# Five small edits to the order of work in a two-layer encoder kernel: pooling products issued later, one split issued a step later, weight splits on two engines, a second PSUM bank for spread scales, and the last two tiles finished in halves

## The chip, the cores and the metric

The kernel runs on one core of one Trainium2 chip. The metric is device time in microseconds of one execution of the whole program, given as the median of three timed runs. The engines carry the names of the profile: PE is TensorE's matmul pipe and PEld its weight load, DVE is VectorE, ACT is ScalarE, POOL is GpSimd, and SP is the queue that issues most transfers.

## The reference, cut to what matters

Two request groups, a prompt of 2048 rows and a sample of 512, pass through the same two layers of width 1024:

```python
h = rms_norm(x, pre_g)
u, zp, q, k, v, za = jnp.split(h @ w_in, SPLIT_POINTS, axis=-1)
pool_out = multiscale_pool(u, pool_w, pool_scale) * silu(zp)   # 4 groups: (window mean - u) @ pool_w[g]
q, k = rope(q), rope(k)
# per head two softmax maps: a = softmax(q0 k0) - lam * softmax(q1 k1); o = a @ v, RMSNorm per head
attn_out = diff_attention(q, k, v, lam, subln_g, lambda_init) * silu(za)
y = jnp.concatenate([pool_out, attn_out], axis=-1) @ w_out
x = x + rms_norm(y, post_g)
```

## The kernel before

Every float32 operand of a product is split into a high part (a copy rounded to the matmul's format, mostly on ACT) and a low part (source minus high part, on DVE or POOL), and products are made of two or three matmuls of parts. The function `split` (L111 the high part, L116 the low part) does both. Each layer has three stages.

**Projection.** `stream` (L279, L251) multiplies 512-row blocks (`hth`, `htl`) by 256-column slices of the weight (`wh`, `wl`), kind by kind in the order u, zp, k, v, q, za, each first for the prompt's blocks 0 and 1, then for 2 and 3. `evacuate` takes results out of PSUM. Every matmul yields to a scheduler, `advance`, which in one of three turns takes a single step of a generator `pool_block`. There are 20 pooling groups in a layer (five blocks, four window sizes), one after the other. A group loads `u` from device memory, adds windows on POOL (tiles `sum`, L367, up to four passes, then edge fixes at L372 and L375), subtracts on DVE (`df`, L379), splits `df` into `dhl` (ACT, then DVE), lets nine steps pass, does three matmuls into PSUM bank `mm` (L387), scales (L390), splits into `hl` and stores. The tiles `u`, `z`, `df` and `dhl` have one buffer each, so the `u` of one group is loaded after the `df` of the group ahead of it is done. When the projection's last matmul for the prompt has been issued, a loop `while q: drop(q)` issues whatever of the pooling generators is left.

**Attention.** Steps of four score products (L442, L443, tiles `sc`), maxima on DVE (L453), exponentials on ACT (L469), combination of the two maps on POOL (L484, L485), transposes on PE with splits (`tr`, `ath`, `atl`, L494), products with v (`ot`, L511). `fill` puts other matmuls in between: the sample's last projections into bank `mm`, then the pooled half of the output projection (L702), whose weights `load_wout` splits when they arrive: rows of 1024 columns, high parts `woh` on ACT, low parts `wol` on DVE for the first four, POOL in halves for the last four. Near the end `fill.first` advances `first_outputs`, which spreads the per-row scales of the first tiles over 128 columns (`spread`, L747), rescales (`rescale`, L751), splits, and starts the attention half of the output projection.

**Output.** `phase3` goes over 20 tiles of 128 rows. For each it spreads scales into bank `mm`, rescales into `mixs`, splits into `hl` (ACT and POOL), multiplies by the output weights (L757), adds to the pooled half (`y`, L803), and `post` normalizes: square sum on ACT (L842), power on POOL (L846), scaling on DVE (L848), residual add on POOL (L850), store. In the last layer the last tile goes through `post_half` in two halves (L819 to L830); the tile ahead of it uses the short pauses `QUICK`.

PE, ACT, DVE and POOL execute in the order in which this code issues (`manual_schedule`); SP's order is chosen by the framework. The eight PSUM banks are four `sc`, two `tr`, one `ot`, one `mm`.

Of the kernel before, what the change touches and what calls it, by code (L numbers as in the profile page):

```python
# [11 lines left out]
F32 = mybir.dt.float32  # L12
# [8 lines left out]
P = 128  # L21
# [3 lines left out]
H = 4  # L25
# [8 lines left out]
FILL = 6  # L34
AGAIN = 2
RAW = 6
FAST = 1
SLOW = 3
LATER = 8
ONE = 2  # L40
# [12 lines left out]
def f32(ap):  # L53
    return ap.bitcast(F32)
# [3 lines left out]
def trunk_kernel(ctx: ExitStack, tc: tile.TileContext, a, outs):  # L58
# [14 lines left out]
    def bank(tag):  # L73

        taken[tag] += 1
        return psum.tile([P, TB], F32, name=f"{tag}{taken[tag] % BANKS[tag]}")
# [272 lines left out]
    def pool_block(c, st, tb, u_p, t_p, tag):  # L349

        S = st["S"]
        for g, w in enumerate(WINDOWS):
            u = u_p.tile([P, TB + 2 * HALO], F32, name="u", bufs=1)
            lo_t, hi_t = tb * TB - HALO, (tb + 1) * TB + HALO
            a0, a1 = max(lo_t, 0), min(hi_t, S)
            if a0 > lo_t:
                nc.gpsimd.memset(u[:, :HALO], 0.0)
            if a1 < hi_t:
                nc.gpsimd.memset(u[:, TB + HALO :], 0.0)
            nc.sync.dma_start(u[:, a0 - lo_t : a1 - lo_t], st["us"][g][:, a0:a1])  # L360
            z = u_p.tile([P, TB], F32, name="z", bufs=1)
            nc.sync.dma_start(z, st["zs"][g][:, tb * TB : (tb + 1) * TB])
            j0, cur, step = HALO - w // 2, u, 1
            while step < w:
                n = TB + w - 2 * step
                nx = u_p.tile([P, TB + 2 * HALO], F32, name="sum")
                nc.gpsimd.tensor_tensor(nx[:, j0 : j0 + n], cur[:, j0 : j0 + n], cur[:, j0 + step : j0 + step + n], op=ALU.add)  # L367
                cur, step = nx, 2 * step
                yield
                yield  # L370
            if a0 > lo_t:
                nc.gpsimd.tensor_tensor(cur[:, j0 : j0 + HALO], cur[:, j0 : j0 + HALO], efix[:, g, :HALO], op=ALU.mult)  # L372
            if a1 < hi_t:
                e0 = j0 + TB - HALO
                nc.gpsimd.tensor_tensor(cur[:, e0 : e0 + HALO], cur[:, e0 : e0 + HALO], efix[:, g, HALO:], op=ALU.mult)  # L375
            yield
            yield
            df = u_p.tile([P, TB], F32, name="df", bufs=1)
            nc.vector.scalar_tensor_tensor(df, cur[:, j0 : j0 + TB], 1.0 / w, u[:, HALO : HALO + TB], op0=ALU.mult, op1=ALU.subtract)  # L379
            yield  # L380
            d = u_p.tile([P, 2, TB], F32R, name="dhl", bufs=1)
            split(d[:, 0], d[:, 1], df, nc.scalar, nc.vector)
            for _ in range(9):
                yield
            ps = bank(tag)
            for i, (pw, m) in enumerate((("pwh", 0), ("pwl", 0), ("pwh", 1))):
                nc.tensor.matmul(ps, lhsT=c[pw][:, g, :], rhs=d[:, m], start=i == 0, stop=i == 2)  # L387
            yield
            mx = u_p.tile([P, TB], F32, name="df", bufs=1)
            nc.vector.scalar_tensor_tensor(mx, ps, c["psc"][:, g : g + 1], z, op0=ALU.mult, op1=ALU.mult)  # L390
            yield
            hl = t_p.tile([P, 2, TB], F32R, name="hl")
            split(hl[:, 0], hl[:, 1], mx, nc.scalar, nc.vector)
            nc.sync.dma_start(st["mp"][:, g, :, tb * TB : (tb + 1) * TB], f32(hl))

    def attention(c, p, po, fill):
# [156 lines left out]
        def block(st, h, qb, ks, vs, q=None):  # L553
            nch = st["S"] // TB
            b = dict(st=st, h=h, qb=qb, ks=ks, vs=vs, q=q or load_q(st, h, qb), sets=[])
            b["z"] = [None, None]
            b["g"] = p["o"].tile([P, QB], F32, name="g", bufs=2)
            nc.sync.dma_start(b["g"], st["gs"][h][:, qb * QB : (qb + 1) * QB])
            for qt in range(2):
                for m in range(2):  # L560
                    b["sets"].append(dict(b=b, qt=qt, m=m, nch=nch, ps=[], e=[]))
            jobs = [(s, ch) for s in b["sets"] for ch in range(nch)]
            for i in range(0, len(jobs), 4):
                yield jobs[i : i + 4]

        def blocks():

            nq, ns = pr["S"] // QB, sa["S"] // QB
            ahead = None
            for h in range(H):  # L570
                kv = load_head(pr, h)
                for qb in range(nq):
                    yield from block(pr, h, qb, *kv[:2], kv[2] if qb == 0 else None)
                    if h == H - 1:
                        n = qb
                        if qb == nq - 1:
                            fill.last()
                        if qb == 0:
                            fill.all()
                            ahead = load_head(sa, 0)  # L580
                        if n % ns == 0:
                            skv = ahead
                        if qb == nq - 1:
                            fill.first(1)
                        yield from block(sa, n // ns, n % ns, *skv)
                        if n % ns == 0 and n // ns + 1 < H:
                            ahead = load_head(sa, n // ns + 1)

# [91 lines left out]
    def load_wout(l, p, wo, ks, raws, pools):  # L680

        for k in ks:
            raw = raws.pop(0)
            wp = p["wop" if k < GROUPS else "woa"]
            wo["h", k] = wp.tile([P, D], F32R, name=f"woh{k}")
            wo["l", k] = wp.tile([P, D], F32R, name=f"wol{k}")
            if k < GROUPS:
                split(wo["h", k], wo["l", k], raw, nc.scalar, nc.vector)
            else:
                for ns in halves:  # L690
                    for _ in range(WGAP):
                        yield
                    split(wo["h", k][:, ns], wo["l", k][:, ns], raw[:, ns], nc.scalar, nc.gpsimd)
            if k + 2 < KT:
                raws.append(load_rows(l, k + 2, pools[k % 2]))
            if k < GROUPS:
                yield
# [48 lines left out]
            wide = st["rstat"][:, t, h : h + 1].to_broadcast([P, P])  # L746
            nc.tensor.transpose(ps[:, h * P : (h + 1) * P], wide, ident)  # L747

    def rescale(ps, src, m, hl, lo_eng):

        nc.vector.tensor_tensor(m, ps.rearrange("p (h n) -> p h n", h=H), src, op=ALU.mult)  # L751
        split(hl[:, 0], hl[:, 1], m, nc.scalar, lo_eng)

    def head_products(ps, hl, wo, ns):
        todo = [(hl[:, m, h, :], wo[w, GROUPS + h]) for h in range(H) for m, w in terms]
# [4 lines left out]
    def phase3(l, wo, scaling, pairs, early, ready, ph, mixed, kept, es, nxt):  # L760
# [22 lines left out]
        def scale(s):  # L783
            if s["hl"] is not None:
                return
            ps = bank("mm")
            spread(ps, s["st"], s["t"])
            yield
            s["hl"] = m_p.tile([P, 2, H, P], F32R, name="hl")
            rescale(ps, s["h"], m_p.tile([P, H, P], F32, name="mixs"), s["hl"], nc.gpsimd)  # L790
            yield

        def products(s):
# [19 lines left out]
        def post_half(s, ns):  # L813

            st, t, y = s["st"], s["t"], s["y"]
            if ns.start == 0:
                s["sy"] = small.tile([P, 2], F32, name="sy2")
            junk = y_p.tile([P, D], BF16, name="junk", bufs=1)
            nc.scalar.activation(junk[:, ns], y[:, ns], AF.Square, accum_out=s["sy"][:, ns.start // TB : ns.start // TB + 1])  # L819
            nc.vector.tensor_tensor(y[:, ns], y[:, ns], gpost[:, ns], op=ALU.mult)  # L820
            yield
            if ns.start:
                ss = small.tile([P, 1], F32, name="sy")
                nc.gpsimd.tensor_tensor(ss, s["sy"][:, 0:1], s["sy"][:, 1:2], op=ALU.add)
                nc.gpsimd.tensor_scalar(ss, ss, 1.0 / D, NORM_EPS, op0=ALU.mult, op1=ALU.add)
                rs = small.tile([P, 1], F32, name="ry")
                nc.gpsimd.tensor_tensor(rs, ss, mhalf[:, :1], op=ALU.pow)
                for ns in halves:
                    nc.vector.scalar_tensor_tensor(y[:, ns], y[:, ns], rs, s["x"][:, ns], op0=ALU.mult, op1=ALU.add)
                    nc.sync.dma_start(st["y"][t * P : (t + 1) * P, ns], y[:, ns])  # L830

        def post(st, t, s):
# [2 lines left out]
                    yield  # L835

            y = s["y"]
            lags = LAGS if nxt or len(tiles) < len(order) or s is not tiles[-2] else QUICK
            yield from pause(lags[0])
            junk = y_p.tile([P, D], BF16, name="junk", bufs=1)  # L840
            ss = small.tile([P, 1], F32, name="sy")
# [44 lines left out]
    class Layer:  # L886
# [60 lines left out]
        def run(self, posts, before):  # L947
# [145 lines left out]
            def first_outputs():  # L1093
# [3 lines left out]
                def prepare(t, m, hl):  # L1097
                    ps = bank("tr")
                    spread(ps, pr, t)
                    rescale(ps, pairs["p", t // 2 * 2 * P][:, :, t % 2 * P : (t % 2 + 1) * P], m, hl, nc.vector)  # L1100
                    ready["p", t] = hl
                    yield

# [123 lines left out]
```

## Time and profile before

| | |
|---|---|
| timed runs | 3168.99, 3148.02, 3166.07 us |
| median | 3166.07 us |
| profiled execution, own time | 3150.91 us |
| its span, first to last instruction | 3149.1 us |
| PE busy in the span | 3065.4 us |
| mean granted TensorE clock | 0.994 |

The profile's span is 1.8 us shorter than the execution's own time. The profiled execution lies near the fastest of the timed runs, 15.2 us below their median. A matmul's row gives a modelled duration, longer than the distance to the next matmul's start when they follow without a wait, so PE's work is counted by starts.

### The profile page before, as it was taken

Reading aid. Unit: us, or ns where it says so; the run is one execution under the profiler, and the core shown is the slowest. Engines: PE = TensorE matmul, PEld = TensorE weight load, DVE = VectorE, ACT = ScalarE, POOL = GpSimd, SP = SyncE. Lnnn points to the kernel's source line nnn. Section 1 sums busy time; section 2 is a strip of 40 time slices with the busy share of each in tenths; the row PEclk is TensorE's granted clock in tenths of the full one; section 3 lists DMA queues with packets and bytes.
Section 4 is the critical chain, followed back from the end, with each engine's and each line's share of the span. In section 5 each row is a group of like instructions: output and inputs, shape, how many; then the busy total and the mean of one; then the engine's idle time right before and its main releaser. Section 6 shows DMA issues by size and latency. Waiting matters only on the chain. (4 is left out here: it accounts for less than half of the span.)

```text
span 3149.1 us, 48450 instructions
## 1 busy us (share of the span) xinstructions
PE 3065.4 (97%) x17016; PEld 2585.4 (82%) x17016; DVE 2069.5 (66%) x3255; ACT 1719.1 (55%) x3915; POOL 1768.4 (56%) x1972
## 2 busy tenths in 40 slices
PE   8999999999998999998999999999999989999998
PEld 6898888778887888887778888897788878888876
DVE  3354255688888887775634543556888888877754
ACT  3244233377777777763333442333777777777632
POOL 1000122289997888885710002222999978878766
PEclk9999999999999999999999999999999999999999
DMA  5354357653424434436854544577424243344367
GB/s 203 116 158 151 124 161 205 197 151 94 124 67 120 122 97 142 128 104 223 307 170 121 158 137 131 170 202 220 134 85 121 65 136 106 108 137 123 101 224 257
DMA packets 298899, 464.53 MB, mean 148 GB/s; under 512 B 26144, under 2 KB 180768, under 8 KB 298656
## 3 DMA queue, kind: packets, MB, share of 16 engines
q1 hardware_dynamic: 292032, 439.42, 46.8%
q10 hardware_dynamic: 6624, 22.02, 1.8%
q8 instruction: 134, 2.20, 0.3%
q14 instruction: 109, 0.89, 0.1%
HBM read 293.57 MB, written 167.77 MB: 146 GB/s over the span
## 5 line engine op out<-in xcount | busy, mean ns | idle before, releaser
L453 DVE TENSOR_REDUCE mx<-sc 128x1 f32<-128x512 f32 x1024 | 650.1, 684 | 185.4 <-PE sc L443 185.2
L469 ACT ACTIVATE e<-sc,nm 128x512 f32<-128x512 f32 x1088 | 732.4, 694 | 32.2 <-DVE nm L456 28.5
L485 POOL TENSOR_TENSOR e<-e,e 128x1024 f32<-128x1024 f32 (+1 forms) x288 | 664.5, 2307 | 24.0
L279 PE MATMUL sc<-hth,wh 128*128 128x512 f32 x1408 | 556.1, 395 | 1.1 <-ACT wh L111 1.0
L279 PE MATMUL sc<-htl,wh 128*128 128x512 f32 x1408 | 554.7, 394 | 0.2 <-DVE htl L116 0.2
L279 PE MATMUL sc<-hth,wl 128*128 128x512 f32 x1408 | 553.2, 393 | 0.5 <-DVE wl L116 0.5
L111 ACT ACTIVATE ath<-tr 128x512 fp32r<-128x512 f32 x544 | 329.3, 606 | 252.1 <-PE ot L511 190.7
L442 PE MATMUL sc<-ks,q 128*128 128x512 f32 x1024 | 433.9, 424 | 3.3 <-ACT e L469 3.1
L443 PE MATMUL sc<-ks,q 128*128 128x512 f32 x1024 | 406.0, 397 | 0.0
L116 DVE TENSOR_TENSOR atl<-tr,ath 128x512 fp32r<-128x512 f32 x544 | 364.9, 682 | 25.7 <-ACT ath L111 25.5
L511 PE MATMUL ot<-ath,v 128*128 128x256 f32 x2176 | 368.7, 291 | 6.7 <-DVE mt L521 6.7
L494 PEld LDWEIGHTS tr<-ident,e 128*128 128x128 f32 x2176 | 266.3, 141 | 98.1 <-DVE atl L116 27.4
L494 PE MATMUL tr<-ident,e 128*128 128x128 f32 x2176 | 328.7, 274 | 18.1 <-DVE atl L116 14.6
L484 POOL TENSOR_SCALAR e<-e,nco 128x1024 f32<-128x1024 f32 (+1 forms) x288 | 329.9, 1145 | 14.9
L169 POOL TENSOR_TENSOR rs<-ss,mhalf 128x1 f32<-128x1 f32 x40 | 25.6, 639 | 552.6 <-DVE ss L167 552.6
L511 PEld LDWEIGHTS ot<-ath,v 128*128 128x128 f32 x2176 | 310.5, 190 | 30.4 <-DVE mt L521 9.2
L279 PEld LDWEIGHTS sc<-hth,wl 128*128 128x128 f32 x1408 | 264.7, 188 | 60.3 <-DVE wl L116 1.1
L279 PEld LDWEIGHTS sc<-hth,wh 128*128 128x128 f32 x1408 | 264.9, 188 | 59.9 <-ACT wh L111 1.4
L279 PEld LDWEIGHTS sc<-htl,wh 128*128 128x128 f32 x1408 | 265.0, 188 | 57.7 <-DVE htl L116 0.5
L442 PEld LDWEIGHTS sc<-ks,q 128*128 128x128 f32 x1024 | 193.8, 189 | 64.7 <-ACT e L469 38.3
L116 DVE TENSOR_TENSOR wl<-wr,wh 128x1024 fp32r<-128x1024 f32 x94 | 121.0, 1289 | 183.0 <-ACT wh L111 183.0
L469 ACT ACTIVATION_READ_ACCUMULATOR e<-sc,nm 128x1 f32 x1088 | 231.5, 213 | 0.0
(156 smaller groups left out, 5725.2 us busy)
## 6 DMA issues: line engine op xcount, KB each, us to landing
wr<-in_w_in SPq DMA_DIRECT2D x128, 512.0 KB, 4.1
q<-qs_p SPq DMA_DIRECT2D x128, 256.0 KB, 4.1
ks_p<-hl SPq DMA_DIRECT2D x64, 256.0 KB, 3.4
vs_p<-hl SPq DMA_DIRECT2D x128, 128.0 KB, 2.5
qs_p<-hl SPq DMA_DIRECT2D x64, 256.0 KB, 3.5
mp_p<-hl SPq DMA_DIRECT2D x32, 512.0 KB, 3.8
ks<-ks_p SPq DMA_DIRECT2D x64, 256.0 KB, 6.0
v<-vs_p SPq DMA_DIRECT2D x32, 512.0 KB, 5.8
```

The costliest lines, as they stand in the source:

```text
L111: nc.scalar.activation(hi, src, AF.Copy)
L116: lo_eng.tensor_tensor(lo, src, f32(hi), op=ALU.subtract)
L169: nc.gpsimd.tensor_tensor(rs, ss, mhalf[:, :1], op=ALU.pow)
L279: nc.tensor.matmul(ps, lhsT=w[k // 4][m][:, k % 4, ns], rhs=h[:, k, :], start=k + i == 0, stop=k == KT - 1 and i == 2)
L442: nc.tensor.matmul(ps, lhsT=q[:, m, 0, ts], rhs=kk, start=True, stop=False)
L443: nc.tensor.matmul(ps, lhsT=q[:, m, 1, ts], rhs=kk, start=False, stop=True)
L453: nc.vector.reduce_max(s["mx"][:, ch : ch + 1], s["ps"][ch], axis=AX.X)
L469: nc.scalar.activation(dst, s["ps"][ch], AF.Exp, bias=s["nm"], accum_out=s["b"]["z"][s["qt"]][:, m, ch : ch + 1])
L484: nc.gpsimd.tensor_scalar(x1[:, :n], x1[:, :n], nco, 0.0, op0=ALU.mult, op1=ALU.add)
L485: nc.gpsimd.tensor_tensor(x0[:, :n], x0[:, :n], x1[:, :n], op=ALU.add)
L494: nc.tensor.transpose(ps[:, j, qt * P : (qt + 1) * P], e[kt // 8][:, kt % 8 * P : (kt % 8 + 1) * P], ident)
L511: nc.tensor.matmul(b["ot"][:, :QB], lhsT=b["vs"][v][kt // 8][:, kt % 8, :], rhs=at[:, j, :], start=unit + i == 0, stop=kt == nkt - 1 and i ...
```

## The change

1. A pooling group lets 13 steps pass between splitting `dhl` and its three matmuls, where it let nine.
2. In `first_outputs` the split after `rescale` is issued one step later (the split is taken out of `rescale`, and a `yield` stands ahead of it). After the sample's last attention block `fill.first(1)` is called once more.
3. The low parts of the first four output weights are made in halves, one on DVE and one on POOL.
4. In `phase3` the spread scales alternate between banks `mm` and `ot`.
5. The last two tiles go through `post_half` (`FAST = 2`), the third from the end takes `QUICK`, and the last but one waits six more steps (`BEFORE`) before its final scaling.

```diff
-FAST = 1
+FAST = 2
+BEFORE = 6
...
             split(d[:, 0], d[:, 1], df, nc.scalar, nc.vector)
-            for _ in range(9):
+            for _ in range(13):
                 yield
...
                         yield from block(sa, n // ns, n % ns, *skv)
+                        if qb == nq - 1:
+                            fill.first(1)
...
-                split(wo["h", k], wo["l", k], raw, nc.scalar, nc.vector)
+                nc.scalar.activation(wo["h", k], raw, AF.Copy)
+                for ns, eng in zip(halves, (nc.vector, nc.gpsimd)):
+                    eng.tensor_tensor(wo["l", k][:, ns], raw[:, ns], f32(wo["h", k])[:, ns], op=ALU.subtract)
...
-    def rescale(ps, src, m, hl, lo_eng):
+    def rescale(ps, src, m):
         nc.vector.tensor_tensor(m, ps.rearrange("p (h n) -> p h n", h=H), src, op=ALU.mult)
-        split(hl[:, 0], hl[:, 1], m, nc.scalar, lo_eng)
...
-            ps = bank("mm")
+            ps = bank(("mm", "ot")[s["t"] % 2])
             spread(ps, s["st"], s["t"])
...
-            rescale(ps, s["h"], m_p.tile([P, H, P], F32, name="mixs"), s["hl"], nc.gpsimd)
+            m = m_p.tile([P, H, P], F32, name="mixs")
+            rescale(ps, s["h"], m)
+            split(s["hl"][:, 0], s["hl"][:, 1], m, nc.scalar, nc.gpsimd)
...
                 nc.gpsimd.tensor_tensor(rs, ss, mhalf[:, :1], op=ALU.pow)
+                for _ in range(0 if s is tiles[-1] else BEFORE):
+                    yield
...
-            lags = LAGS if nxt or len(tiles) < len(order) or s is not tiles[-2] else QUICK
+            lags = LAGS if nxt or len(tiles) < len(order) or s is not tiles[-1 - FAST] else QUICK
...
-                    rescale(ps, pairs["p", t // 2 * 2 * P][:, :, t % 2 * P : (t % 2 + 1) * P], m, hl, nc.vector)
+                    rescale(ps, pairs["p", t // 2 * 2 * P][:, :, t % 2 * P : (t % 2 + 1) * P], m)
+                    yield
+                    split(hl[:, 0], hl[:, 1], m, nc.scalar, nc.vector)
```

Line numbers grow by one to five in the changed kernel. On PE, the end of the projection stage and the first scores (`sc<-ks,q`) stood like this before, the same in both layers; the last three pooling matmuls (`mm<-dhl`) are 61 projection matmuls further up.

```order
L279 MATMUL sc_5244<-hth,wl 128x512
L279 MATMUL sc_5244<-hth,wh 128x512
L279 MATMUL sc_5244<-htl,wh 128x512
L279 MATMUL sc_5244<-hth,wl 128x512
L442 MATMUL sc_5338<-ks,q 128x512
L443 MATMUL sc_5338<-ks,q 128x512
```

In the changed kernel the matmuls of the last three of the 20 groups stand between the last projection matmul and the first score.

```order
L280 MATMUL sc_5167<-hth,wl 128x512
L388 MATMUL mm_5209<-dhl,pwh 128x512
L388 MATMUL mm_5209<-dhl,pwl 128x512
L388 MATMUL mm_5209<-dhl,pwh 128x512
L388 MATMUL mm_5238<-dhl,pwh 128x512
L388 MATMUL mm_5238<-dhl,pwl 128x512
L388 MATMUL mm_5238<-dhl,pwh 128x512
L388 MATMUL mm_5269<-dhl,pwh 128x512
L388 MATMUL mm_5269<-dhl,pwl 128x512
L388 MATMUL mm_5269<-dhl,pwh 128x512
L443 MATMUL sc_5338<-ks,q 128x512
L444 MATMUL sc_5338<-ks,q 128x512
```

So three groups moved past the end of the stage; the group ahead of them (`mm_5130`) stands 37 projection matmuls further up. On POOL, at the same place before, the windows of the last two groups (`sum`) follow each other, and the three low parts of the sample's first projection weights (`wl`) come behind them.

```order
L367 TENSOR_TENSOR sum<-u 128x518
L367 TENSOR_TENSOR sum<-sum 128x516
L367 TENSOR_TENSOR sum<-sum 128x512
L372 TENSOR_TENSOR sum<-sum,efix 128x8
L375 TENSOR_TENSOR sum<-sum,efix 128x8
L357 MEMSET u 128x8
L359 MEMSET u 128x8
L367 TENSOR_TENSOR sum<-u 128x526
```

In the changed kernel one of these `wl` stands ahead of those windows, and another two groups further up.

```order
L117 TENSOR_TENSOR wl<-wr,wh 128x1024
L358 MEMSET u 128x8
L360 MEMSET u 128x8
L368 TENSOR_TENSOR sum<-u 128x518
L368 TENSOR_TENSOR sum<-sum 128x516
L368 TENSOR_TENSOR sum<-sum 128x512
```

So the last two groups' windows now queue behind a weight split. On ACT, near the end of attention, the high part of the first tile's rescaled rows (`wor<-yo`) stood ahead of a step's four exponentials before.

```order
L111 ACTIVATE ath<-tr_15877 128x512
L111 ACTIVATE wor<-yo 128x512
L469 ACTIVATE e_15926,zc<-sc_15844,nm 128x512
L469 ACTIVATE e_15926,zc<-sc_15859,nm 128x512
L469 ACTIVATE e_15946,zc<-sc_15864,nm 128x512
L469 ACTIVATE e_15946,zc<-sc_15870,nm 128x512
```

In the changed kernel it stands behind them and the step's two transposes, ahead of the next step's exponentials.

```order
L470 ACTIVATE e_15948,zc<-sc_15874,nm 128x512
L731 ACTIVATE yo<-mm_15835 128x512
L112 ACTIVATE ath<-tr_15932 128x512
L520 ACTIVATE sq<-ot_15706 128x256
L112 ACTIVATE ath<-tr_15958 128x512
L112 ACTIVATE wor<-yo 128x512
L470 ACTIVATE e_16010,zc<-sc_15925,nm 128x512
```

The exponentials therefore no longer stand behind that split; the split's low part on DVE moved in the same way.

## The prediction

> **What bounds the kernel now.** I read the page's first lines first.
>
> ```profile
> span 3149.1 us, 48450 instructions
> PE 3065.4 (97%) x17016; PEld 2585.4 (82%) x17016; DVE 2069.5 (66%) x3255; ACT 1719.1 (55%) x3915; POOL 1768.4 (56%) x1972
> ```
>
> PE works nearly always, and the change neither adds nor removes a matmul. So it can only take away PE's waits or add some. Of the view of who waited for whom on PE (total, times, longest), these rows belong to the edits:
>
> ```profile
> PE tr L494 <- DVE atl L116: 14.6, 15, 2.3
> PE mm L387 <- ACT dhl L111: 5.8, 4, 2.3
> PE mm L747 <- DVE mixs L751: 4.3, 4, 2.1
> PE sc L442 <- DVE wor L116: 4.2, 2, 2.1
> ```
>
> All four together are 28.9 us, 0.9% of the span, and only a part of the first is within reach. A wait costs more than itself where the granted clock (first number after the bracketed counts) falls:
>
> ```profile
> 978.00:988.00 10.00, 7.65 (x39) 6.22 (x38) 9.11 (x13) 6.22 (x16) 7.00 (x8) 0.83 0.31 91
> 1535.00:1552.00 17.00, 13.42 (x60) 10.87 (x60) 13.87 (x17) 7.08 (x12) 14.18 (x12) 0.90 0.65 212
> 2063.00:2072.00 9.00, 7.21 (x43) 6.53 (x43) 4.35 (x7) 3.38 (x7) 0.70 (x2) 0.81 0.85 211
> ```
>
> Each stretch holds one wait near 2 us, and behind it some 3.4 us at half clock: 10 x 0.17, 17 x 0.10, 9 x 0.19, each 1.7 us of matmul time.
>
> **Edit 1, later pooling products: a gain inside the stage, a larger loss at its end.** The gain is the row of L387, 5.8 us. Four more turns of three matmuls are 2.8 us, longer than the longest of these waits (2.3). The stretch from 2063 holds one of them, so 1.7 us of clock go too: 7.5 us.
>
> The loss is in the moved rows on PE. Twenty groups, each four turns longer, no longer fit into the stage, and the matmuls of the last three stand ahead of the first score with nothing between them. Before, the last group's matmuls started 61 matmuls earlier, and the scores followed at once:
>
> ```profile
> 616.55 0.39 PE L387 MATMUL mm<-dhl,pwh 128*128 128x512 f32 x1
> 630.74 0.40 PE L279 MATMUL sc<-hth,wl 128*128 128x512 f32 x1
> 630.98 0.39 PE L442 MATMUL sc<-ks,q 128*128 128x512 f32 x1
> ```
>
> 62 starts in 14.43 us give 0.233 us a matmul. Those 61 covered the chain of a group; that cover is gone. I take the chain from its last instance:
>
> ```profile
> 598.69 0.68 DVE L379 SCALAR_TENSOR_TENSOR df<-sum,u 128x512 f32<-128x512 f32 x1
> 605.45 1.06 POOL L367 TENSOR_TENSOR sum<-u 128x526 f32<-128x526 f32 x1 [5.87 <-DMA u<-us_s]
> 606.59 4.79 POOL L367 TENSOR_TENSOR sum<-sum 128x524 f32<-128x524 f32 x3
> 611.61 0.20 POOL L375 TENSOR_TENSOR sum<-sum,efix 128x8 f32<-128x8 f32 x1
> 572.12 0.69 DVE L116 TENSOR_TENSOR dhl<-df,dhl 128x512 fp32r<-128x512 f32 x1 [0.70 <-ACT dhl L111]
> u<-us_s SPq DMA_DIRECT2D x8, 256.0 KB, 3.2
> ```
>
> The first subtraction frees `u`, only then does the next `u` come in, POOL adds its windows, and only then does the next subtraction start. Let t = 0 be the third matmul of the first sample group (`mm_5130`). The 37 projection matmuls behind it end at 8.9, the second group's third matmul starts at 9.3. Without waits the scores would start at 8.9 + 9 x 0.233 = 11.0. On POOL the third group's windows stand behind a weight split, which waits for ACT:
>
> ```profile
> 625.63 0.60 ACT L296 ACTIVATE rb<-sc 128x512 f32<-128x512 f32 x1 [4.51 <-PE sc L279]
> 629.28 2.41 POOL L116 TENSOR_TENSOR wl<-wr,wh 128x1024 fp32r<-128x1024 f32 x1 [15.11 <-ACT wh L111]
> 587.87 1.49 POOL L367 TENSOR_TENSOR sum<-u 128x518 f32<-128x518 f32 x1 [4.43 <-DMA u<-us_s]
> 592.83 0.65 POOL L375 TENSOR_TENSOR sum<-sum,efix 128x8 f32<-128x8 f32 x1
> ```
>
> Here the split starts 3.65 us after the evacuation `rb`. In the changed order that evacuation follows 13 matmuls behind t = 0, at 3.5, so the split runs from 7.15 to 9.55 (the third `u` has landed by 9.2: subtraction of the second group at 5.9, plus 0.1 to issue and 3.2). Windows of the third group: 5.6 (587.87 to 593.48), to 15.2. Subtraction 0.7, high part 0.65, low part 0.75 with the handover: its third matmul at 17.3. The fourth group's `u` leaves at 16.0 and is there at 19.2; windows 6.4 (605.45 to 611.81), to 25.6; subtraction, high and low part 2.1: third matmul at 27.8, scores at 28.1. That is **17.1 us of idle PE in each layer**, in gaps of about 7 and 10 us. Behind them I put 2.3 us of half clock (the stretches above show 1.7 behind a wait of 2 us; a long gap may cost two such spells, 3.4). 2 x (17.1 + 2.3) = **+38.8 us**.
>
> Bounds: had the windows been ready, a drained group would still need scaling, subtraction and split behind the matmuls ahead of it, from 572.12 in the trace:
>
> ```profile
> 573.41 0.75 DVE L390 SCALAR_TENSOR_TENSOR df<-mm,psc,z 128x512 f32<-128x512 f32 x1 [0.59 <-PE mm L387]
> 575.28 0.68 DVE L116 TENSOR_TENSOR hl<-df,hl 128x512 fp32r<-128x512 f32 x1
> ```
>
> 0.55 + 0.75 + 0.65 + 0.7 + 0.7 + 0.65 + 0.75 = 4.75 us, so 9.5 for two groups, 8.4 more than before: the short end is 2 x 8.4 = 16.8. At the long end `u` lands in 5.8 us twice (the slowest in the view of the tile `u`) and the clock costs 3.4: 2 x (17.1 + 5.2 + 3.4) = 51.4.
>
> [...]
>
> **Edit 2, the split a step later.** PE's scores need the first exponential, which on ACT stands behind the split's high part, which waits for the rescale:
>
> ```profile
> 1419.28 0.63 ACT L111 ACTIVATE wor<-yo 128x512 fp32r<-128x512 f32 x1 [2.90 <-DVE yo L751]
> 1419.82 0.67 ACT L469 ACTIVATE e<-sc,nm 128x512 f32<-128x512 f32 x1
> 1420.63 0.50 PE L442 MATMUL sc<-k,q 128*128 128x512 f32 x1 [2.11 <-DVE wor L116]
> ```
>
> With the split behind the four exponentials these are ready earlier and both waits go, 4.2 us. The split's 0.63 us of ACT then stand ahead of the next step's exponentials, with its reader several us away. I take -4.2 (ends -2 and -6).
>
> **Edit 3, four weights' low parts on two engines.**
>
> ```profile
> 1003.15 2.38 POOL L485 TENSOR_TENSOR e<-e,e 128x1024 f32<-128x1024 f32 x1
> 1003.24 3.38 DVE L116 TENSOR_TENSOR wol<-wor,woh 128x1024 fp32r<-128x1024 f32 x1
> 1007.28 0.66 PE L494 MATMUL tr<-ident,e 128*128 128x128 f32 x4 [2.31 <-DVE atl L116]
> L116 POOL TENSOR_TENSOR wol<-wor,woh 128x512 fp32r<-128x512 f32 x16 | 21.4, 1339 | 18.1 <-ACT woh L111 18.1
> 988.48 0.48 POOL L478 TENSOR_TENSOR zc<-zc 128x4 f32<-128x4 f32 x2 [3.23 <-ACT e L469]
> ```
>
> DVE's split crawled beside POOL's addition and held up the transposes. A half saves about 0.6 us (0.7 for 512 columns in the rows above), and at this place perhaps the whole 2.3, since POOL's two halves (1.34 each) now push that addition behind it. POOL pays by starting combinations 1 to 3 us later; the idle 3.23 us take some of it. Between a gain of 2 x 2.9 = 5.8 and a loss of 2.8 I take -4.0, nearest to the row of the 2.31 us wait.
>
> [...]
>
> **Edit 4, two banks.** A spread waited for the rescale ahead of it to read the one bank:
>
> ```profile
> 1544.87 0.86 PE L747 MATMUL mm<-ident,rstat_s 128*128 128x128 f32 x4 [2.09 <-DVE mixs L751]
> ```
>
> With `ot` free at that stage the waits go: 4.3, with 1.7 of clock from the stretch at 1535: -6.0. What is late next is the four `sc` banks, emptied by DVE; they hold two tiles, so I expect no wait there (end: 0 if it moves there).
>
> **Edit 5, the end.** PE is done here; DVE and POOL alternate:
>
> ```profile
> 3133.89 2.37 POOL L850 TENSOR_TENSOR y<-y,xr 128x1024 f32<-128x1024 f32 x1 [1.40 <-DVE y L848]
> 3139.92 1.53 DVE L820 TENSOR_TENSOR y<-y,gpost 128x512 f32<-128x512 f32 x1 [0.84 <-ACT junk L819]
> 3141.37 0.68 DVE L803 TENSOR_TENSOR y<-sc,y 128x512 f32<-128x512 f32 x1
> 3144.59 1.41 DVE L829 SCALAR_TENSOR_TENSOR y<-y,ry,xr 128x512 f32<-128x512 f32 x2 [0.99 <-POOL ry L827]
> ```
>
> From 3133.7 on the new DVE order has an addition, a product that waits for POOL's residual (3136.8), an addition, 0.9 for the square, a product, an addition, 0.9, a product, two scalings of the last but one (1.4), and only then the last addition, at 3142.4 where it was 3141.37. One residual addition of POOL is saved, but not on this path: +1.0 (ends -2 and +3).
>
> **The sum.** +38.8 - 7.5 - 4.2 - 4.0 - 6.0 + 1.0 = **+18.1 us**. The profiled execution took 3150.91 us itself (span 3149.1), so 3169.0 on its level. The median of the runs is 3166.07, so 3184 there; that is my number, slower by 0.6%. A measurement here can tell about 1% from no change.
>
> **Rivals.**
> *The end of the stage is drained quickly* (the other side). If the windows of the last groups are ready when their turn comes, the drain costs 16.8 in all, and the sum is -3.9: 3162. It turns the sign below 10 us a layer. For it: POOL is nearly idle in this stage. Against it: the single `u` buffer, and POOL's row above that waited 5.87 us for `u`. Chance 0.15.
> *The drain is hidden altogether*, because the changed order does not bite in time: only the gains less 1.0, -20.7, about 3145. Against it: nothing on PE stands between those matmuls and the scores. 0.10.
> *The drain is dearer*: `u` comes late behind the key loads that SP now issues between, and the clock stays low for two spells, 51.4, while edits 3 and 4 bring nothing (gains 11.7, less 1.0): +40.7, 3207. It passes 1% from 26 us a layer on. For it: loads of 256 KB stand between the `u` loads now. 0.20.
> *Likeliest*, as summed: 0.55. That edit 1 fails to do what it says, the waits for `dhl` staying as they are, would add 7.5 to any of these.
>
> **Range and chances.** From 3150 (the drain near its short end, with runs at the level of the profiled execution or the quickest, 3148.02) to 3206 (the dear drain). Faster by over 1% would need more than every gain here: 0.02. Slower by over 1%: the dear drain, 0.20. Within 1%: 0.78.
>
> **What would show it.** In the changed profile: two PE gaps of about 7 and 10 us behind L388 shortly after 620 us, and again in layer two, with a granted clock below 1 after them; POOL waiting there for `u<-us_s`; no PE wait of L443 on `wor`, and none of the spread on `mixs`; the waits on `dhl` inside the stage gone. I am wrong if the gaps are below 5 us, or if edits 2 to 4 bring back more than 20 us.

## The result, and the profile after

The changed kernel takes 3171.57 us in the median of 20 runs (3166.60 to 3182.97), the kernel before 3148.65 us in 20 runs (3145.46 to 3172.80): a ratio of **1.0061, with a 95% interval of 1.0047 to 1.0074**. It is slower, by about the 0.6% that was forecast (the two medians alone differ by 22.9 us, 0.7%). The profiled execution of the changed kernel took 3168.76 us itself; on that level the forecast was 3169.0. The number on record, 3184, stood on a median of three runs (3166.07), and the 17 later runs put that 17 us lower.

The first lines of the page after. PE's matmul count is what it was (17016) and its busy time within 1 us (3065.4 before); the span is 17.5 us longer, so no work was added, and the loss is waiting or clock.

```profile
span 3166.6 us, 48486 instructions
PE 3064.4 (97%) x17016; PEld 2586.9 (82%) x17016; DVE 2070.3 (65%) x3258; ACT 1719.9 (54%) x3917; POOL 1765.9 (56%) x1980
```

Who waited for whom on PE after the change (total, times, longest):

```profile
PE mm L388 <- ACT dhl L112: 25.8, 4, 7.9
PE tr L495 <- DVE atl L117: 12.4, 15, 2.2
PE tr L179 <- DVE htl L117: 9.5, 7, 3.5
PE tr L752 <- DVE atl L117: 5.3, 2, 2.7
PE sc L252 <- DVE wl L117: 1.5, 2, 0.8
```

The wait for `dhl`, 5.8 us before with 2.3 as the longest, is now 25.8 us in four pieces. The rows on `wor` (4.2) and `mixs` (4.3) are gone as forecast, but the third, fourth and fifth row carry waits that are longer (6.1, 2.1 and 0.3 before).

To see where the 17.5 us arise, the same matmul is looked up in both timelines (start, duration, line, operation). The places are, in order: early in the projection, the first `mm` fill of the attention stage, the first score of the sample, then the same in layer two, and the last matmul. Before:

```profile
155.16 0.28 PE L251 MATMUL sc<-wh,hth 128*128 128x256 f32 x1
632.95 0.39 PE L279 MATMUL mm<-hth,wh 128*128 128x512 f32 x1
1202.86 0.40 PE L442 MATMUL sc<-k,q 128*128 128x512 f32 x1
1719.67 0.28 PE L251 MATMUL sc<-wh,hth 128*128 128x256 f32 x1
2197.41 0.39 PE L279 MATMUL mm<-hth,wh 128*128 128x512 f32 x1
2769.01 0.40 PE L442 MATMUL sc<-k,q 128*128 128x512 f32 x1
3134.39 0.39 PE L757 MATMUL sc<-wol,hl 128*128 128x512 f32 x1
```

After:

```profile
156.42 0.28 PE L252 MATMUL sc<-wh,hth 128*128 128x256 f32 x1
646.62 0.39 PE L280 MATMUL mm<-hth,wh 128*128 128x512 f32 x1
1215.94 0.40 PE L443 MATMUL sc<-k,q 128*128 128x512 f32 x1
1729.56 0.28 PE L252 MATMUL sc<-wh,hth 128*128 128x256 f32 x1
2220.26 0.39 PE L280 MATMUL mm<-hth,wh 128*128 128x512 f32 x1
2789.03 0.40 PE L443 MATMUL sc<-k,q 128*128 128x512 f32 x1
3149.99 0.39 PE L761 MATMUL sc<-wol,hl 128*128 128x512 f32 x1
```

The lag of the changed kernel at these places is 1.26, 13.67, 13.08, 9.89, 22.85, 20.02 and 15.60 us, and 17.5 at the end of the span. The differences give a ledger by stage:

| stretch | edits in it | measured | forecast |
|---|---|---|---|
| start | none | +1.3 | 0 |
| rest of the two projection stages | 1 | +12.4 and +13.0 | +31.3 |
| attention up to the sample's scores, two layers | 3 | -0.6 and -2.8 | -4.0 |
| from there to the end of the matmuls, two layers | 2 and 4 | -3.2 and -4.4 | -10.2 |
| behind the last matmul | 5 | +1.9 | +1.0 |

A stretch also holds the half-clock spells that happened to fall into it (granted clock 0.50 for 3.41 us each in both traces, so up to 1.7 us). In the third row there were 1 and 2 such spells before and 1 and 1 after, in the fourth 3 and 1 before and 2 and 0 after, so up to 1.7 of the 3.4 us and up to 3.4 of the 7.6 us there are clock. In the third row PE's idle time (length of the stretch less PE's busy time) fell by 1.6 and 1.7 us.

The drain, that is the matmuls of the last three groups issued in one piece at the stage's end, in layer one on the changed kernel's timeline. PE's rows are the third matmul of the first sample group, the stage's last projection matmul, the last matmul of the second group, both ends of the third and of the fourth, and the first score:

```profile
617.08 0.39 PE L388 MATMUL mm<-dhl,pwh 128*128 128x512 f32 x1
625.70 0.40 PE L280 MATMUL sc<-hth,wl 128*128 128x512 f32 x1
627.24 0.51 PE L388 MATMUL mm<-dhl,pwh 128*128 128x512 f32 x1 [0.67 <-DVE dhl L117]
632.78 0.80 PE L388 MATMUL mm<-dhl,pwh 128*128 128x512 f32 x1 [5.04 <-ACT dhl L112]
633.80 0.63 PE L388 MATMUL mm<-dhl,pwh 128*128 128x512 f32 x1
642.26 0.80 PE L388 MATMUL mm<-dhl,pwh 128*128 128x512 f32 x1 [7.83 <-ACT dhl L112]
643.28 0.63 PE L388 MATMUL mm<-dhl,pwh 128*128 128x512 f32 x1
643.70 0.63 PE L443 MATMUL sc<-ks,q 128*128 128x512 f32 x1
```

```profile
624.24 2.40 POOL L117 TENSOR_TENSOR wl<-wr,wh 128x1024 fp32r<-128x1024 f32 x1 [6.04 <-ACT wh L112]
624.71 2.47 DVE L117 TENSOR_TENSOR dhl<-df,dhl 128x512 fp32r<-128x512 f32 x1 [1.71 <-ACT dhl L112]
626.79 1.29 POOL L368 TENSOR_TENSOR sum<-u 128x518 f32<-128x518 f32 x1
631.29 0.69 DVE L380 SCALAR_TENSOR_TENSOR df<-sum,u 128x512 f32<-128x512 f32 x1 [1.37 <-POOL sum L376]
635.30 1.06 POOL L368 TENSOR_TENSOR sum<-u 128x526 f32<-128x526 f32 x1 [3.12 <-DMA u<-us_s]
640.77 0.69 DVE L380 SCALAR_TENSOR_TENSOR df<-sum,u 128x512 f32<-128x512 f32 x1 [3.85 <-POOL sum L376]
```

With t = 0 at 617.08, POOL's weight split starts at 7.16 (forecast 7.15), the third group's last matmul at 16.7 (17.3), the fourth's at 26.2 (27.8), the first score at 26.6 (28.1). The scores would have come at 11.0 without waits, so they are 15.6 us late. The granted clock of that stretch (first number after the bracketed counts) stands at half:

```profile
629.00:646.00 17.00, 5.39 (x12) 3.73 (x13) 6.58 (x9) 2.71 (x5) 7.36 (x12) 0.50 0.72 201
```

It stays there until 646, some two us into the scores. The nine matmuls that start from 642.26 on in that time need 0.43 us each in place of 0.233, so some 1.8 us are clock, 0.7 of them ahead of the first score; nearly all the rest of the delay is idle PE.

### The profile page after: what moved, and what is told of

Read it like the earlier page. It is cut to its first block, busy times and chain, and to the rows that moved or that the text cites. A ratio compares the mean times of both kernels' runs of the same rounds, so it can differ in the third digit from the quotient of the medians.

```text
span 3166.6 us, 48486 instructions
## 1 busy us (share of the span) xinstructions
PE 3064.4 (97%) x17016; PEld 2586.9 (82%) x17016; DVE 2070.3 (65%) x3258; ACT 1719.9 (54%) x3917; POOL 1765.9 (56%) x1980
## 5 line engine op out<-in xcount | busy, mean ns | idle before, releaser
L495 PE MATMUL tr<-ident,e 128*128 128x128 f32 x2176 | 328.3, 274 | 14.1 <-DVE atl L117 12.4
```

Of the source, the lines that this page charges most:

```text
L495: nc.tensor.transpose(ps[:, j, qt * P : (qt + 1) * P], e[kt // 8][:, kt % 8 * P : (kt % 8 + 1) * P], ident)
```

## The experiments

All are timed in the same way as the change; kernels of one group ran on one chip with the kernel before beside them, whose median there is given. These medians of one and the same kernel lie between 3148.65 and 3153.57 us, so a difference of a few us between kernels of two groups is not settled by the times, and the traces, one of each kernel, have to help. "Theory" is that the drain of the last pooling groups is the loss.

### Edit 1 alone, and everything but edit 1 (before: 3153.57)

```diff
-            for _ in range(9):
+            for _ in range(13):
```

> Edit 1 alone on the kernel before. Theory (the loss is the drain: the matmuls of three groups stand between the last projection matmul and the first score, 15.6 us later scores in each layer, and it is the only loss of size): the waits of 5.3 and 8.2 us stay in both layers, the waits for dhl inside the stage go (5.8 us and one half-clock spell of 1.7), so about +25 us on the kernel before, ratio 1.008, more than the whole change. Rival (edits 2 to 5 cost part of what was lost, and edit 1 pays for some of its drain elsewhere): +17 us or less, ratio 1.0055 or below.

3177.21 us, ratio 1.0075 [1.0058, 1.0091]. PE's wait for `dhl` in it is that of the changed kernel to the tenth, and the wait on `wor`, which edit 2 removes, is still there (line numbers of before):

```profile
PE mm L387 <- ACT dhl L111: 25.8, 4, 7.9
PE sc L442 <- DVE wor L116: 4.2, 2, 2.1
```

By the ledger's places the two projection stages are 13.3 and 13.0 us longer; the start is 2.1 us longer, and everything else within 1 us.

The changed kernel with nine steps again:

> The changed kernel with edit 1 undone (nine steps again). Theory: no drain, scores follow the projection at once; the waits for dhl are back; edits 2 to 5 are worth what the two traces show stage by stage, about 5 (edit 2), 3.4 (edit 3), 2 (edit 4) and -2 (edit 5), so some 8 us below the kernel before, ratio 0.9975. Rival (edits 2 to 5 cost): ratio 1.000 or above.

3143.62 us, ratio 0.9966 [0.9954, 0.9979]. So edit 1 costs more than the whole change, and edits 2 to 5 together bring about 10 us. Theory as expected; the rival is out.

### How many groups are drained: ten and eleven steps (same chip)

> The changed kernel with ten steps. By the issue order the last group's matmuls then stand one matmul ahead of the first projection's end, and none is drained. Theory (it is the drained groups that cost, not the steps): no wait behind the projection above 2 us, time within 3 us of the kernel with nine. Rival (each step more costs its share of some 33 us, whatever the order at the end): +8 us on the kernel with nine.

> The changed kernel with eleven steps: one group is drained, 13 matmuls behind the group ahead of it. Theory: its windows can be added while the group ahead still waits for its turn, so only the short chain counts (scaling, subtraction, split, 4.75 us, less 3.7 us of matmuls in between): a wait of 1 to 5 us in each layer, 2 to 13 us in all on the kernel with ten. Rival (each drained group costs the same third of 33 us): +11 us, in gaps of about 5 us each. Rival by steps: +8 us on the kernel with ten.

Ten steps: 3144.12 us, ratio 0.9973 [0.9958, 0.9988], the same as with nine, so it is not the steps that cost. Its profiled execution was slower, 3153.82 us, and in its trace a score behind the projection waits 2.74 us for an exponential, where no wait above 2 us was expected; that one trace lost 11.3 us in layer one's attention stage. Eleven: 3154.70 us, ratio 1.0000 [0.9986, 1.0015], 10.6 us more. Here the theory's size was wrong: the drained group cost a gap of 7.0 us in each layer, not 1 to 5. The time is that of the rival by groups (+11 us), though its gaps were to be 5 us. The trace of eleven steps shows why. The rows are the load of that group's `u`, and POOL's work:

```profile
613.25 0.32 SPq L361 DMA_DIRECT2D u<-us_s  x1
624.34 2.39 POOL L117 TENSOR_TENSOR wl<-wr,wh 128x1024 fp32r<-128x1024 f32 x1 [11.85 <-ACT wh L112]
626.90 1.31 POOL L368 TENSOR_TENSOR sum<-u 128x526 f32<-128x526 f32 x1
```

`u` is loaded 10 us ahead of the windows, and POOL idles 11.85 us, because a weight split that waits for ACT stands ahead of the windows in its order.

### Eleven steps with that weight split on DVE (before: 3149.78)

```diff
             if jobs[j][3] == "sc":
                 return load_w(raw, p, nc.scalar, nc.vector)
+            if jobs[j - 1][3] == "sc":
+                return load_w(raw, p, nc.scalar, nc.vector, later)
```

> Edits 2 to 5 with eleven steps, and the low parts of the two weight halves that are split on POOL at the end of the projection stage made on DVE. With eleven steps one group is drained; its u was issued at 613.25 us in the trace, but POOL's windows began at 626.90, behind a weight split that stood ahead of them in POOL's order and waited 11.85 us for ACT. Theory (that split, not the load of u, holds the drained group): the windows are done before the group's turn, only scaling, subtraction and split are left, 4.75 us less 3 us of projection matmuls; the gap falls from 7.0 us to 2 us or less in each layer, some 10 us in all, near 3144. Rival (DVE's own order or the load sets the gap): above 5 us as before, no change in time.

3144.80 us, ratio 0.9984 [0.9971, 0.9998]: below the kernel with the split on POOL, by 9.9 us in the medians of the two groups, by 5 us in the ratios; in the traces the two projection stages are 5.1 and 6.1 us shorter. The windows now start when `u` lands, and the gap is 2.4 us, a little over the 2 that were expected:

```profile
619.07 1.06 POOL L370 TENSOR_TENSOR sum<-u 128x526 f32<-128x526 f32 x1 [6.41 <-DMA u<-us_s]
```

```profile
629.53 0.50 PE L390 MATMUL mm<-dhl,pwh 128*128 128x512 f32 x1 [2.24 <-ACT dhl L112]
```

So for one drained group the price was set by what stood ahead of it in POOL's in-order queue, and the quick drain of the rivals is what is left when that is taken away. With three drained groups the edit was not run.

### Two buffers for `u` (before: 3150.00)

```diff
-            u = u_p.tile([P, TB + 2 * HALO], F32, name="u", bufs=1)
+            u = u_p.tile([P, TB + 2 * HALO], F32, name="u", bufs=2)
```

> The changed kernel (thirteen steps) with two buffers for the tile u in place of one. Theory (in the drain the fourth group's windows wait for its u, which is loaded only when the third group's subtraction has freed the one buffer): the windows of the fourth group follow those of the third at once, 4.05 us sooner in each layer, so the second gap falls from 8.2 us to about 4.2 and the first stays near 5.3 (its windows stand behind POOL's weight split); some 8 us below the changed kernel, ratio to before near 1.0035. Rival (POOL's or DVE's own order sets the gap, the load is hidden): gaps of 5.3 and 8.2 us as they are, ratio 1.006.

3175.20 us, ratio 1.0074 [1.0056, 1.0092]: not faster. The drain did what the theory said: the first gap is as it was, the second 5.1 us in place of 8.2, since the fourth group's windows follow at once on the third's. Rows of the kernel with two buffers, waits first, then the timeline:

```profile
PE mm L388 <- ACT dhl L112: 19.5, 4, 5.0
PE sc L252 <- ACT wh L112: 5.1, 2, 2.9
PE sc L252 <- DVE wl L117: 3.2, 2, 1.6
```

```profile
637.72 1.49 POOL L368 TENSOR_TENSOR sum<-u 128x526 f32<-128x526 f32 x1
```

The 6.3 us saved on `dhl` are given back in the middle of the projection, where PE waits 8.3 us for a weight's parts (1.9 without this edit). In that stretch of layer one POOL now adds the windows of a wider group (526 columns from 500.98 on, without this edit 518 from 499.40 on), and ACT waits 3.64 us for a store of k in place of 1.76; what made the store late was not separated.

### Single edits undone, from the kernel with edits 2 to 5

Edit 3 undone (before: 3150.00):

> Edits 2, 4 and 5 alone: nine steps, and edit 3 undone as well (low parts of the first four output weights whole on DVE). Theory: the time rises by what the stage between the first pooled output products and the last sample scores showed, 3.4 us on the kernel with edits 2 to 5, and a wait of 2.3 us stands before the transposes again. Rival (DVE's and POOL's halves only lock each other out, and the gain came from elsewhere): no change or faster by up to 2 us.

3144.16 us, ratio 0.9966 [0.9950, 0.9982]. Median and ratio cannot tell it from the kernel with edits 2 to 5 (0.9966 as well). In the traces it has lost 2.2 us by the sample's scores of layer one and 1.1 more in layer two, about the 3.4 expected, and the 2.31 us wait before the transposes is back in layer one. But that stage holds 1 and 2 half-clock spells in its trace and none in the other, and these can make up all of the difference. So what the halves are worth is open between nothing and 3.4 us.

That DVE's and POOL's halves hold each other up shows in the changed kernel's trace, layer one. DVE's four took 1.42, 0.94, 2.88 and 0.68 us and POOL's 1.28, 1.27, 1.72 and 1.29; DVE's first began 0.41 us behind POOL's and ended 0.55 us behind it, and POOL's 1.72 is the one beside DVE's 2.88, which stood beside POOL's addition before that. Whole on DVE, in the kernel before, they took 1.22, 1.59, 1.21 and 3.38 us, the 3.38 beside POOL's addition.

Edit 5 undone (before: 3150.00):

> Edits 2, 3 and 4 alone: nine steps, and edit 5 undone as well. Theory (the last addition on DVE comes 8.8 us behind the last matmul in place of 7.0): 1.8 us below the kernel with edits 2 to 5; 14.7 us from the start of the last matmul to the end of the span, in place of 16.6. Rival (POOL's residual addition, which the old tail has once more, eats it): no change.

3140.49 us, ratio 0.9971 [0.9953, 0.9989]. By the medians that is 3 us below the kernel with edits 2 to 5 on another chip, by the ratios (0.9966 there) no gain, so the times do not decide. Its trace has 14.4 us from the last matmul's start to the end, near the 14.7 expected, in place of 16.6 in the changed kernel and 17.4 in the one with edits 2 to 5.

Edit 4 undone (before: 3148.71):

> Edits 2, 3 and 5 alone: nine steps, and edit 4 undone as well (all spread scales in bank mm). Theory (in layer one the removed wait only moved to the next layer's transposes, because DVE is late there by itself): the two waits on mixs of 1.6 and 2.1 us come back and the wait on htl of 3.7 us behind them goes, layer one ends at the same time within 0.5 us; layer two's output stage is 1 to 1.5 us longer; so 1 to 2 us above the kernel with edits 2 to 5. Rival (edit 4 is worth its predicted sum): 6 us above.

3146.00 us, ratio 0.9997 [0.9984, 1.0010]: by the medians 2.4 us above the kernel with edits 2 to 5 on another chip, by the ratios 10 us. In layer one the waits change places. With one bank:

```profile
1541.25 0.65 PE L752 MATMUL mm<-ident,rstat_s 128*128 128x128 f32 x4 [2.10 <-DVE mixs L756]
1550.35 0.93 PE L752 MATMUL mm<-ident,rstat_s 128*128 128x128 f32 x4 [2.04 <-DVE mixs L756]
```

With two banks (the kernel with edits 2 to 5):

```profile
1547.69 1.12 PE L179 MATMUL tr<-ident,xt 128*128 128x128 f32 x4 [3.45 <-DVE htl L117]
```

Three waits on `mixs` of 1.4 to 2.1 us, or one on `htl` of 3.45 and one on `y` of 1.8: PE is ahead of DVE there, and waits at the next thing DVE makes. By the places the edit is worth some 1.9 us in layer one (where the trace with one bank has a half-clock spell more) and 1.4 in layer two. The traces speak against the rival's 6 us; the times, which disagree by that much, do not rule them out.

### More steps only where PE waited

```diff
-            for _ in range(9):
+            for _ in range({(0, 2, 3): 13, (1, 0, 0): 11}.get((int(st is sa), tb, g), 9)):
```

On edits 2 to 5 (before: 3150.00):

> Edits 2 to 5 with thirteen steps only for the group that waited 2.2 us for dhl (prompt block 2, widest window), eleven for the one that waited 0.9 us (sample, narrowest window), nine for the other eighteen. By the issue order no group is drained. Theory: the 6.1 us of these waits and one half-clock spell of 1.7 us go without the drain: about 7 us below the kernel with edits 2 to 5, near 3136. Rival (the wait moves to the next group, or PE's lead is lost at the start of attention, as with ten steps): no change to -2 us.

3139.67 us, ratio 0.9960 [0.9944, 0.9975]: the lowest ratio of all, but only 4 us below the kernel with edits 2 to 5 by the medians and 2 by the ratios, not 7. On the kernel before (before: 3148.71):

> Edit 1 alone on the kernel before, for two groups only (thirteen steps for prompt block 2's widest window, eleven for the sample's narrowest, nine for the rest); no group is drained. Theory: the four waits for dhl (5.8 us) go, with up to one half-clock spell of 1.7: 6 to 7.5 us below the kernel before, ratio 0.998. Rival (PE's lead is spent at the first attention steps, where the next transfers and exponentials set the end): -3 us or less.

3147.55 us, ratio 0.9993 [0.9984, 1.0002]: 1 us, not 6. Here the rival holds. The waits on `dhl` are gone in both, and in their place stand these (first kernel):

```profile
PE sc L280 <- DVE wl L117: 2.8, 4, 1.3
PE sc L280 <- ACT wh L112: 2.0, 3, 0.8
PE sc L443 <- DMA ks<-ks_p: 1.9, 3, 0.9
```

PE that no longer waits for `dhl` reaches the next weight, and at the stage's end the first keys, before they are ready.

With the old tail as well (before: 3148.71):

> Edits 2, 3 and 4 with edit 1 for two groups only (thirteen steps for prompt block 2's widest window, eleven for the sample's narrowest, nine for the rest) and the tail of before. Theory: what the selective steps and the old tail showed adds up, 1.8 us below the kernel with edits 2 to 5 and selective steps, near 3138, ratio 0.9955. Rival (the time is set by how many half-clock spells an execution happens to meet, and the single gains drown in them): within 2 us of either of the two kernels.

3141.04 us, ratio 0.9978 [0.9969, 0.9987]. It adds nothing that can be measured; the three best kernels (this one, the selective one and the one with edits 2 to 4) lie within 1.4 us. All of them beat both kernels of the case.

## Why the prediction was right, point by point

**The sign, the place and the mechanism of the loss** were right: three groups drained ahead of the scores, two gaps (5.3 and 8.2 us where 7 and 10 were forecast), half clock behind, and no other loss of size. The sum (+18.1) and the span (+17.5) agree more closely than the terms do.

**Edit 1** was forecast at +31.3 and measured +25.4 (26.3 alone). The drain was put at 19.4 us a layer. Measured it is the ledger's +12.4 and +13.0 with the gain inside the stage added back. That gain is read at the stage's last projection matmul, in layer one at 630.74 before, behind 60 pooling matmuls, and at 625.70 after, behind 51. Nine matmuls less are 2.1 us, and the changed kernel came 1.26 us late into the stage, so 4.2 us were gained. In layer two the rows are these, the lag there was 9.89, and the gain is 3.6. Before, then after:

```profile
2195.20 0.40 PE L279 MATMUL sc<-hth,wl 128*128 128x512 f32 x1
```

```profile
2199.34 0.40 PE L280 MATMUL sc<-hth,wl 128*128 128x512 f32 x1
```

So the drain cost 16.6 us in each layer, 15.6 of them ahead of the first score in layer one: 2.8 less than forecast. About half of that is the half clock behind the first score (1.0 in place of 2.3), and the other half lies ahead of it. There the term that was too large is the windows: 5.6 and 6.4 us were taken from rows beside which DVE was busy for 5.5 and 1.9 us; in the drain it was busy for 1.8 and 1.0, and they took 4.5 (626.79 to the subtraction at 631.29) and 5.5 (635.30 to 640.77). That DVE made the difference was not tested. Against it, the second group was 0.9 us later than forecast, since its low part took 2.47 us beside POOL's weight split. That the third group would stand behind that split, and the fourth behind the load of `u`, was right; the experiments with the split moved (one group drained) and with two buffers each showed one of them.

The gain inside the stage, forecast at 7.5, came to 7.8. The step "what is late next" was left out of it: where the waits on `dhl` went, PE waited 0.75 us in layer one and 1.2 in layer two for `wl` and `wh`. It came out all the same because a wait delays PE by more than its idle time (the one of 2.25 us at 501.64 by 3.0, counted in starts of the same matmuls). Among the bounds, the short end's 8.4 us a layer comes to 8.1 from its own rows (9.5 less six matmuls), which changes no chance.

**Edit 2** was forecast at -4.2. With edit 4 it makes -7.6, so about -4.3 once edit 4's 3.3 are taken off; up to 3.4 of the 7.6 are the two spells fewer, and no run undoes edit 2 alone. The waits themselves show less: the wait on `wor` went (2 x 2.1), part of it came back at the next transposes (2 x 2.7 on `atl`; before, there were waits of 1.0 there and of 1.2 behind), so about 3 us of idle time went in both layers together.

**Edit 3** was -4.0 forecast; both pairs of traces show about -3.4, but with one and with three half-clock spells fewer, so its worth is not settled.

A low part on DVE took longer beside POOL's work in the drain too: the one started at 624.71 took 2.47 us, where the 38 of that tile outside the two drains took 0.69 to 0.70, and ended at 627.18, 0.54 us behind POOL's split (to 626.64). That the halves lose by this did not come in sight: both pairs differ the other way.

**Edit 4** failed in the step "what is late next": not the `sc` banks but `htl`, because DVE itself is late at the turn to layer two. By the traces it is worth 3.3 us, halfway between the lower end named, "0 if it moves", and the -6.0.

**Edit 5** was +1.0, measured +1.9 in this pair, for the reason given: the last addition comes 8.8 us behind the last matmul's start in place of 7.0. Over all traces the stretch behind the last matmul is 1.0 to 2.7 us longer than in the kernel before in the nine with edit 5, and -0.4 to 0.9 in the four others.

**The clock.** The drain brought the half clock in both layers (0.50 for 17.07 us from 628.95 on and again from 2202.49 on). The spells behind short waits were counted as if each such wait had one. They do not come each time: the wait of 2.13 us at 980.75 in the kernel before had one (0.83 in that stretch); the same wait in the kernel with edits 2 to 5 had none:

```profile
981.37 0.66 PE L495 MATMUL tr<-ident,e 128*128 128x128 f32 x4 [2.13 <-DVE atl L117]
```

```profile
979.00:989.00 10.00, 7.51 (x47) 6.00 (x46) 9.65 (x16) 7.59 (x18) 7.90 (x9) 1.00 0.32 89
```

The drain and these waits differ as far as certainty goes: the drain's gaps of 5 and 8 us came with the half clock in both layers of the changed kernel and in layer one with edit 1 alone (0.56 from 629 to 646), the waits of 2.1 to 2.2 us for `atl` in 20 of 28 instances.

So the forecast was right in size partly by luck, because two errors offset: edit 1 was 5.9 us cheaper than forecast, edits 2 to 5 brought 4.1 us less, and 1.3 us came at the start of the kernel, where nothing was changed.

## What to carry to other kernels

When steps are added between a producer and its consumer in an order that is advanced by turns, count the turns in the stage: what no longer fits is issued at its end in one piece, and there its whole chain stands on the path. The price of such a drain is read from the in-order queues of the helpers, so look for the one instruction that stands ahead of the drained work and waits for something else (POOL's weight split with eleven steps, behind 11.85 us of idle time). A short wait that is removed is worth its length only if the next operand is ready (the selective steps took 6 us of waits away and brought 1 us alone, 2 to 4 us on edits 2 to 5); look up which row of the waits that one is in.

## What the hardware showed that was not expected

- **Whether a short wait brought the half clock went by where it fell.** Over the 14 traces, the 28 instances of the wait of 2.1 to 2.2 us for `atl` (one in each layer) were followed by a spell of half clock in 20, counted in stretches of 10 us. In each trace all spells begin on one grid of 3.413 us (to within 5 ns; in the kernel before, the spells at 981.97 and 1459.83 are 140 steps apart), and the grid lies differently in each execution (in the changed kernel's, with spells at 994.18 and 1472.04, 0.58 of a step off that one). Of some 12,600 grid steps at full clock, none in which PE idled less than 1.4 us in all was followed by a spell, and each of the 77 with more than 1.94 us was; of the 72 between, 22 were. In the kernel before, the wait of 2.13 us (978.62 to 980.75) lies within one step (978.56 to 981.97). In the kernel with edits 2 to 5 a grid line at 980.04 cuts it into 0.80 and 1.33 us, and no spell came. A spell costs 1.7 us of matmul time (3.41 us at 0.50), and the traces have between three and ten of them outside the drains. As an estimate from these numbers, seven spells are 12 us, so they alone can spread the runs of one kernel by several us and hide edits of 2 to 3 us in the medians.
- **One execution lost 16 us behind waits of 0.6 us.** The profiled execution with selective steps and the old tail took 3155.02 us, 14 us above its median. Up to 800 us it is level with the selective kernel; then a score waits 0.61 us for an exponential (at 810.19) and another 0.62 us for keys (at 816.81), and for the two blocks that follow DVE and POOL fall into another rhythm. First this trace, then the selective kernel, about the same work in both:

```profile
800.00:930.00 130.00, 117.27 (x674) 99.67 (x673) 110.62 (x173) 86.52 (x220) 107.68 (x115) 0.95 0.36 92
```

```profile
800.00:914.00 114.00, 112.18 (x680) 95.26 (x679) 100.69 (x174) 87.01 (x220) 107.93 (x110) 1.00 0.38 105
```

  DVE needs 110.6 us for 173 instructions in place of 100.7 for 174 (third pair), and four spells of half clock come with it. What began it was not tested; the 11.3 us that the trace of ten steps lost arose in the same stage, behind waits for exponentials and for the loaded `q` (1.57 us), not for keys.
